# LRU half of the output projection: two pairs of tiles by seven quarter products over heads 0 to 3, and six conv tiles parked in DRAM

## Chip, cores, metric

The kernel runs on one core of a Trainium2 chip. The metric is the device time of one execution in microseconds (us), lower is better. Times before and after are medians of several runs; the profile is one further execution.

## The reference

One layer of a decoder trunk with 1024 channels and 1024 tokens (batch 1), in float32:

```python
mod = c_act @ mod_w[l] + mod_b[l]; shift, scale, gate = split(mod, 3)
h = rmsnorm(x, norm_g[l]) * (1.0 + scale) + shift
cv, cg, cs, lx, ls = split(h @ w_in[l], 5)              # five blocks of 1024 columns
v = cv * sigmoid(cg)
conv = (silu(layernorm(causal_depthwise_conv(v, 31 taps))) @ pw2 + pw2_b) * silu(cs)
xr = causal_depthwise_conv(lx, 4 taps)
r, i = sigmoid(xr_head @ wr_head + br), sigmoid(xr_head @ wi_head + bi)   # 8 heads of 128
h_t = a_t * h_{t-1} + sqrt(1 - a_t**2) * (i_t * xr_t)   # a_t from r_t, over the tokens
y = h * silu(ls)
x = x + (1 + gate) * (concat(conv, y) @ w_out)          # w_out: 2048 x 1024
out = rmsnorm(x, final_g)
```

The change concerns `y @ w_out[1024:]`, the half of the output projection that the LRU (recurrent) heads feed.

## The kernel before

**Layout.** Channels lie on the 128 partitions, tokens along the free dimension, so an activation of 1024 channels is eight tiles of 128 x 1024. A float32 product is three TensorE terms: each operand is split into a rounded high part (type fp32r) and the remainder (low part), and high x high, high x low and low x high are accumulated in PSUM. One output tile (128 channels x 1024 tokens) takes 8 contraction tiles x 3 terms x 2 halves of 512 tokens, 48 matmuls.

**Order.** All work is given to a planner (`class Plan`) as operations with an engine, a cost, a priority (about the slot number in which they are wanted) and the tiles that they read and write. It simulates the engines and writes out a fixed, in-order instruction stream for each: TensorE (PE), ScalarE (ACT), VectorE (DVE), GpSimd (POOL, which issues the accumulating DMAs) and SyncE (SP, which issues all other DMAs). Nothing is reordered at run time. An engine that waits holds up all that is behind it in its own stream. Tiles come from pools: 47 buffers of 128 x 1024 (`big`), two each for a raw weight tile (`raw`) and its high and low parts (`whi`, `wlo`), three PSUM tiles of 128 x 1024 and two of 128 x 512. A pool's buffer is handed on when its last reader is done.

**Stages.** After a start stage come 40 input tiles (`slots`, one slot each, 48 matmuls), between which eight gate groups stand. Meanwhile DVE, ACT and the accumulating DMAs (`es<-cq`, `oo<-co`) make the depthwise convolution of the conv tiles c0 to c7. Slots 40 to 47 are the eight `lru` tiles: TensorE multiplies the tile's weights with the eight heads (`yh`, `yl` are the high and low parts of y, contraction index k = head), DVE adds the gated result to x (`acc<-ps,gate,acc`, line 379 by way of a helper `STT`), and SP parks it in DRAM (`accd`). In the same stretch the layer norm of the conv tiles runs: `conv_sum` adds c0 to c7 into `csum` in the order `SUMS`, some by accumulating DMAs (`ADD`) and the last `CSD` ones by DVE (`TT`); `csum` is split into `csh` and `csl`, whose product with ones gives `mean`; then each tile has the mean subtracted, is squared into `lnss`, and scaled by `lnbc`. The next stage, `pw2`, is made in pairs of tiles by `pair_products`, with seven quarter products in place of eight, and so is the `out` stage that follows it.

**Weights of the LRU tiles.** `weights` loads a tile (`raw`) on SP 2.5 slots ahead; ACT rounds it to `whi`. From slot 41 on (`LATE`) the low part is made by `remainder`, which is ACT writing -whi to `wlo` and POOL issuing a DMA that adds the float32 weights from DRAM to it:

```python
ACT(prio, lo, lambda: hi().bitcast(F32), AF.Copy, n, scale=-1.0, r=rk, w=wk)
ADD(prio, lo, src, n, r=[*wk, *sk], w=wk, flight=LAND)
```

A tile's matmuls are issued by `mm_k`, one operation for each k. The functions named and their lines follow.

Of the kernel before, what the change touches and what calls it, by code (L numbers as in the profile page):

```python
# [9 lines left out]
F32 = mybir.dt.float32  # L10
F32R = mybir.dt.float32r
# [44 lines left out]
HOLDS = ()  # L56
LASTS = ((0, 3), (0, 1), (0, 1), (0, 3))
BCM = (512, 768)
QDMA = (('y',0,'T2'),('y',1,'T2'))
# [15 lines left out]
WOUT = ("DVE", "DVE", "DVE", "DVE")  # L75
AP = {0: (), 512: (1, 3, 5), 768: (1, 3, 5, 7)}
NP = {0: (6, 0, 1), 512: (6, 0, 7), 768: (6, 0)}
SUMS = (2, 3, 0, 1, 7, 4, 5, 6)
CSD = 4
EVN = 4  # L80
CQR = 2
YHEADS, YSLOT = 2, 36
QRES = 0
SINGLE = (0,)
AHEAD = 4
# [230 lines left out]
def hymba_layer(ctx: ExitStack, tc: tile.TileContext, xT, vecs, mod_w, w_first, w_in,  # L316
# [97 lines left out]
    def big_buf(name, dt=F32, parts=1):  # L414
        return S.buf("big", name, dt, parts)
# [38 lines left out]
    slots = list(FIRST + NEXT)  # L454
    for x in ORDER.split():
        slots.append(("gate" if x[0] == "g" else "in", int(x[1:])))
    slots += [("lru", m) for m in range(KT)]
    wslots = [s for s in slots if s[0] != "gate"] + [("out", m) for m in (4, 5, 6, 7)]
    number = {s: n for n, s in enumerate(wslots)}
    B0, C0, D0 = 40, 48, 56  # L460

# [10 lines left out]
    def k3(b):  # L472
        return lambda: b().rearrange("p (k c) -> p k c", k=KT)

    def remainder(prio, lo, hi, src, n, rk, wk, sk=()):
        ACT(prio, lo, lambda: hi().bitcast(F32), AF.Copy, n, scale=-1.0, r=rk, w=wk)
        ADD(prio, lo, src, n, r=[*wk, *sk], w=wk, flight=LAND)

    def w_slice(s, k, nk, p_load, p_prep, first_load=(), eng="POOL", late=()):
# [22 lines left out]
        w_bufs(s, where)  # L502
        w_slice(s, 0, KT, n - 2.5, n - 1.4, after, eng, late)

    def mm_k(prio, ps, s, xh, xl, k, cols, off=0, nk=KT, after=()):
        wh, wl = whi[s], wlo[s]

        def emit():
            for lhs, rhs, last in ((wh, xh, 0), (wh, xl, 0), (wl, xh, 1)):
                for a, b in cols:  # L510
                    pe.matmul(ps()[:, a - off:b - off], k3(lhs)()[:, k, :], rhs[k]()[:, a:b],  # L511
                              start=(k == 0 and lhs is wh and rhs is xh
                                     and (a - off) % H == 0),
                              stop=(k == nk - 1 and bool(last)), skip_group_check=True)
        n = sum(b - a for a, b in cols)
        rd = [(wh, k), (wl, k)]
# [645 lines left out]
    waiting = []  # L1162
    yh, yl = [None] * KT, [None] * KT

    def gw_load(i, n):
# [12 lines left out]
    def evac_in(m, ps, n, b=None, rb=()):  # L1178
        pr = n + 0.5
        kind, i = (m // KT) * KT, m % KT  # L1180
        if kind == CG:
            sig[i] = big_buf(f"sig{i}")
            ACT(pr, sig[i], ps, AF.Sigmoid, r=[ps], w=[sig[i]])
        elif kind == CV:
            sg = sig.pop(i)
            v[i] = big_buf(f"v{i}")
            TT(pr, "DVE", apart(v[i], 0, T), by_two(ps, 0, T), by_two(sg, 0, T), ALU.mult,
               r=[ps, sg], w=[v[i]])
        elif kind == CS:
            t = big_buf(f"scs{i}")  # L1190
            ACT(pr, t, ps, AF.Silu, bias=b, r=[ps, *rb], w=[t])
            scs_d[i] = dram.tile([P, T], F32, tag=f"scs{i}", name=f"scsd{i}")
            DMA(pr, lambda: scs_d[i], t, FULL_BYTES, r=[t], w=[("scsd", i)])
        elif kind == LS:
            sls[i] = big_buf(f"sls{i}")
            return ACT(pr, sls[i], ps, AF.Silu, bias=b, r=[ps, *rb], w=[sls[i]])
        else:
            xs, xh, xl = (big_buf(f"{a}{i}", d) for a, d in
                          (("xs", F32), ("xsh", F32R), ("xsl", F32R)))

            def w(s):
                o = SCW + i * STAPS + STAPS - 1 - s
                return V[:, o:o + 1]
            ACT(pr, xs, ps, AF.Identity, scale=w(0), bias=vec("sc_b", i), r=[ps], w=[xs])
            for s in range(1, STAPS):
                STT(pr, part(xs, s, T), part(ps, 0, T - s), w(s), part(xs, s, T), ALU.mult,
                    ALU.add, T - s, r=[ps, xs], w=[xs])
            split(pr + 0.2, xh, xl, xs)
            lru[i] = (xs, xh, xl)

    def gates(i, n):
        xs, xh, xl = lru[i]
        hi, lo = gw.pop(i)
        r, g, a = big_buf(f"r{i}"), big_buf(f"g{i}"), big_buf(f"a{i}")
        for j, (dst, b) in enumerate(((r, "br"), (g, "bi"))):
            ps = mm_tile(f"gate{i}_{j}")

            def emit(j=j, ps=ps):
                for lhs, rhs, st in ((hi, xh, 0), (hi, xl, 1), (lo, xh, 2)):
# [12 lines left out]
        TT(pr, "DVE", xs, xs, r, ALU.mult, r=[xs, r], w=[xs])  # L1232
        S.op("DVE", 2.2, lambda: dve.tensor_tensor_scan(
            out=r(), data0=a(), data1=xs(), initial=0.0, op0=ALU.mult, op1=ALU.add),
            pr, [a, xs], [r])
        t = sls.pop(i)
        TT(pr, "DVE", t, t, r, ALU.mult, r=[t, r], w=[t])
        yh[i], yl[i] = big_buf(f"yh{i}", F32R), big_buf(f"yl{i}", F32R)
        o = split(B0 - 2 + 0.2 * i, yh[i], yl[i], t, reserve=SPARE)
        if i < YHEADS:  # L1240
            waiting.append(o)

    def gate_mod(j, n, after):
        mod_load(2 * KT + j, n - 1, after)
# [304 lines left out]
```

## Time and profile before

| | |
|---|---|
| median of 3 runs | 731.97 us (731.78 to 733.33) |
| profiled execution | 731.52 us, span 729.70 us |
| granted TensorE clock | 0.997 |
| busy PE / DVE / ACT / POOL | 721.4 / 611.5 / 460.0 / 145.9 us |

The profile is one execution, recorded by the hardware. Its span runs from the first to the last recorded instruction; the execution's own time is 1.82 us longer. PEld is TensorE's weight load, which overlaps its matmuls. "x<-y" is an operation that writes x from y, by the names in the program with buffer numbers left out; `L379` is a line of the kernel, and where a helper issues all operations of a kind, all of them have the helper's line.

### The profile page before, as it was taken

To read this page: it belongs to the slowest core of one execution; us is meant where nothing else is said; L and a number is where in the kernel's file an instruction comes from. 1 tells how busy PE (TensorE), PEld (TensorE's weight loads), DVE (VectorE), ACT (ScalarE), POOL (GpSimd) and SP (SyncE) were. 2 spreads that over 40 slices of the span, in tenths; PEclk is the share of its full clock that TensorE was granted. 3 is DMA by queue.
4 is the path that set the end of the run, shared out by engine and by line. 5 is a ranking of instruction groups with operands and counts; after the bars stand their busy time and mean duration, and the time that the engine had idled before them with its cause. 6 is when DMAs were issued, how large, how long until landed. Compare 5 with 4: busy or idle time off the path is not lost.

```text
span 729.7 us, 8957 instructions
## 1 busy us (share of the span) xinstructions
PE 721.4 (99%) x3292; PEld 600.3 (82%) x3292; DVE 611.5 (84%) x835; ACT 460.0 (63%) x580; POOL 145.9 (20%) x144
## 2 busy tenths in 40 slices
PE   9999999999999999999999999999999999999996
PEld 8888888888888888888888888888888888888885
DVE  7999999799789997588599999677986566999647
ACT  7650677456698958956859778545953345755322
POOL 0043012353443232232122111000000001010003
PEclk9999999999999999999999999999999999999998
DMA  9943023457899999899576744676566756784006
GB/s 335 407 170 122 0 102 65 98 114 162 193 226 211 258 234 217 174 230 212 109 165 131 156 101 124 177 203 178 161 175 176 216 121 137 217 214 181 16 15 217
DMA packets 40940, 122.61 MB, mean 168 GB/s; under 512 B 4544, under 2 KB 13248, under 8 KB 40896
## 3 DMA queue, kind: packets, MB, share of 16 engines
q0 software_dynamic: 15984, 45.27, 34.2%
q1 hardware_dynamic: 23904, 75.84, 30.9%
q10 hardware_dynamic: 1008, 0.92, 0.4%
q8 instruction: 26, 0.43, 0.2%
q14 instruction: 18, 0.15, 0.1%
HBM read 72.55 MB, written 12.58 MB: 117 GB/s over the span
## 4 chain that ended last, share of the span: by engine, by line
PE 95%; DMA 2%; ACT 1%; DVE 1%; POOL 0%; issue 0%; DVEq 0%; POOLq 0%
PE ps L511 62%; PE xpw L680 6%; PE xout L680 6%; PE first L807 5%; PE ypw L680 3%; PE gate L1221 3%; PE y L655 2%; PE zout L680 1%; PE zpw L680 1%; DMA wlo<-in_w_out_dram 1%; PE yout L680 1%; DMA es<-cq 1%; PE late L807 1%; DVE o L379 1%; PE token_stats L764 1%; ACT cq L368 0%
## 5 line engine op out<-in xcount | busy, mean ns | idle before, releaser
L511 PE MATMUL ps<-uh,whi 128*128 128x512 f32 x576 | 177.5, 389 | 0.1
L511 PE MATMUL ps<-ul,whi 128*128 128x512 f32 x576 | 177.4, 389 | 0.0
L511 PE MATMUL ps<-uh,wlo 128*128 128x512 f32 x576 | 177.3, 389 | 0.0
L511 PEld LDWEIGHTS ps<-uh,whi 128*128 128x128 f32 x576 | 108.0, 188 | 22.8 <-ACT scs L368 0.5
L511 PEld LDWEIGHTS ps<-ul,whi 128*128 128x128 f32 x576 | 108.1, 188 | 22.5
L511 PEld LDWEIGHTS ps<-uh,wlo 128*128 128x128 f32 x576 | 108.1, 188 | 22.5
L360 ACT CAST whi<-raw 128x1024 fp32r<-128x1024 f32 x44 | 45.8, 1047 | 62.9 <-PE ps L511 34.6
L392 POOL DMA_DIRECT2D es<-cq x45 | 42.4, 957 | 117.5 <-ACT cq L368 93.5
L387 POOL TENSOR_TENSOR wlo<-raw,whi 128x1024 fp32r<-128x1024 f32 x16 | 40.8, 2561 | 123.4 <-ACT whi L360 90.7
L368 ACT ACT_TABLE_LOAD x44 | 56.5, 1283 | 2.5 <-issue 1.0
L379 DVE SCALAR_TENSOR_TENSOR cacc<-v,V,cacc 128x511 f32<-128x511 f32 (+14 forms) x75 | 55.4, 739 | 0.3
L379 DVE SCALAR_TENSOR_TENSOR caccs<-v,V,caccs 128x511 f32<-128x511 f32 (+6 forms) x70 | 52.0, 743 | 1.1
L379 DVE SCALAR_TENSOR_TENSOR caccs<-c,wsum,caccs 128x511 f32<-128x511 f32 (+6 forms) x70 | 51.9, 741 | 0.6
L392 POOL DMA_DIRECT2D oo<-co x39 | 36.3, 947 | 72.1 <-ACT co L368 30.3
L511 PE MATMUL ps<-yh,wlo 128*128 128x512 f32 x128 | 39.5, 390 | 0.2 <-DMA wlo<-in_w_out_dram 0.2
L511 PE MATMUL ps<-yh,whi 128*128 128x512 f32 x128 | 39.6, 391 | 0.0
L511 PE MATMUL ps<-yl,whi 128*128 128x512 f32 x128 | 39.5, 389 | 0.0
L368 ACT ACTIVATE cq<-v,V 128x511 f32<-128x511 f32 (+14 forms) x45 | 31.8, 707 | 0.0
L379 DVE SCALAR_TENSOR_TENSOR xs<-ps,V,xs 128x1023 f32<-128x1023 f32 (+2 forms) x24 | 30.6, 1274 | 0.0
L387 DVE TENSOR_TENSOR wlo<-raw,whi 128x1024 fp32r<-128x1024 f32 x21 | 25.6, 1218 | 5.7 <-ACT whi L360 5.6
L368 ACT ACTIVATE cq<-c,wsum 128x512 f32<-128x512 f32 x42 | 29.7, 711 | 0.0
L379 DVE SCALAR_TENSOR_TENSOR modw<-modw,sc 128x1024 f32<-128x1024 f32 x23 | 29.5, 1285 | 0.2 <-DMA modw<-in_mod_w_dram 0.2
(335 smaller groups left out, 1449.0 us busy)
## 6 DMA issues: line engine op xcount, KB each, us to landing
raw<-in_w_in_dram SPq DMA_DIRECT2D x36, 512.0 KB, 4.6
modw<-in_mod_w_dram SPq DMA_DIRECT2D x24, 512.0 KB, 8.5
scsd<-scs SPq DMA_DIRECT2D x8, 512.0 KB, 5.8
raw<-in_w_out_dram SPq DMA_DIRECT2D x8, 512.0 KB, 4.0
accd<-acc SPq DMA_DIRECT2D x8, 512.0 KB, 4.1
rawpw<-in_pw_dram SPq DMA_DIRECT2D x8, 512.0 KB, 4.5
scsr<-scsd SPq DMA_DIRECT2D x8, 512.0 KB, 4.8
rawout<-in_w_out_dram SPq DMA_DIRECT2D x8, 512.0 KB, 3.6
```

The source lines that it names most:

```text
L360: act.copy(out(), in_())
L368: act.activation(out=out(), in_=in_(), func=func, **kw)
L379: dve.scalar_tensor_tensor(out=out(), in0=in0(), scalar=scalar, in1=in1(), op0=op0, op1=op1, accum_out=accum)
L387: lambda: e.tensor_tensor(out=out(), in0=a(), in1=b(), op=op), prio, r, w,
L392: return S.op("POOL", ISSUE, lambda: pool.dma_start(out(), a(), accum_op=ALU.add), prio, r, w, lag=RATE * n / T, after=after, flight=flight)
L511: pe.matmul(ps()[:, a - off:b - off], k3(lhs)()[:, k, :], rhs[k]()[:, a:b], start=(k == 0 and lhs is wh and rhs is xh and (a - off) % H == 0),
L655: pe.matmul(to(), half(*lhs)()[:, j * P:j * P + P], half(*rhs)()[:, c0:c1], start=a == "S1" and j == 0 and t == 0, stop=j == KT // 2 - 1 a ...
L680: pe.matmul(half(ps, 0)(), half(*lhs)()[:, j * P:j * P + P], half(*rhs)(), start=start and j == 0 and t == 0, stop=j == KT // 2 - 1 and t ...
L764: pe.matmul(psb()[:, :P], ones, ones, start=True, stop=True)
L807: pe.matmul(ps()[:, a - off:b - off], fw_part(lhs, k, i * P, i * P + P)(), rhs()[:, a:b], start=k == 0 and lhs is wh and rhs is xh, stop=k ...
L1221: pe.matmul(ps()[:, c0:c1], lhs()[:, j, :], rhs()[:, c0:c1], start=st == 0, stop=st == 2)
```

## The change

The LRU tiles 0 to 3 are no longer four plain tiles but two pairs. Within a pair, the contraction over heads 4 to 7 stays plain. The contraction over heads 0 to 3 is seen as a 2 x 2 block product: weights A11, A12 (first tile of the pair, heads 0 and 2, heads 1 and 3) and A21, A22 (second tile), activations B11, B12 (heads 0 and 2, tokens 0 to 511 and 512 to 1023) and B21, B22 (heads 1 and 3). It is made from seven products of 6 matmuls instead of eight: A11 B11, A12 B21, S1 T1, S2 T2, S3 T3, S4 B22, A22 T4, where S are sums of weight blocks and T sums of activation blocks. `lru_sums` makes T in place from y (four half subtractions on DVE for each pair of heads j) and splits it again into high and low parts; for j = 1 the low parts go by `remainder`, that is by ACT and an accumulating DMA. `lru_pair` loads both tiles, makes S in the raw tiles (four additions or subtractions of 128 x 256 on DVE), splits S (`ls`), and issues the products in the order `LORDER`: p and q, r are the plain parts (24, 12 and 12 matmuls; p for both halves of tile 0 into PSUM `lp`, q for half 1 of tile 1 into `ly`, r for its half 0 into `lx`), and 1, z, y, 2, 3, s, 4 are the seven products. A product that several outputs share is read from PSUM while it stands in its accumulator, each time by one `STT` of 128 x 512 on DVE: eight for a pair. On the host the rows of the LRU half of `w_out` are put in the order `LK`.

To find room for the sums, six conv tiles (`SPILL`) are stored to DRAM by SP when they are complete (`cd`) and loaded again (`cr`) after slot 39 has begun. The order `SUMS` is another, and two conv tiles instead of four are added to `csum` by DVE, five instead of three by accumulating DMAs. The splits of heads 2 and 3, as those of 0 and 1 before, are held until slot 36 (`YHEADS`). `lru` tiles 4 to 7 and all other stages are issued as before.

The diff, with the unchanged middle of `mm_k` and a few small lines left out:

```diff
@@ -75,11 +75,17 @@
 WOUT = ("DVE", "DVE", "DVE", "DVE")
 AP = {0: (), 512: (1, 3, 5), 768: (1, 3, 5, 7)}
 NP = {0: (6, 0, 1), 512: (6, 0, 7), 768: (6, 0)}
-SUMS = (2, 3, 0, 1, 7, 4, 5, 6)
-CSD = 4
+SUMS = (2, 0, 4, 3, 1, 6, 7, 5)
+CSD = 2
+SPILL, SPP0, SPP1, SPN = (0, 2, 4, 3, 1, 6), 30, 40.5, 39
 EVN = 4
 CQR = 2
-YHEADS, YSLOT = 2, 36
+YHEADS, YSLOT = 4, 36
+JS, LRU_P = (0, 1), 2
+NJ = len(JS)
+LK = tuple(2 * j + z for z in (0, 1) for j in JS) + tuple(k for k in range(KT) if k // 2 not in JS)
+LORDER = "p1zy2q3s4r"
+LTP, LTD, LWD = 0.2, (2,1), ()
 QRES = 0
 SINGLE = (0,)
 AHEAD = 4
@@ -454,8 +460,8 @@
     slots = list(FIRST + NEXT)
     for x in ORDER.split():
         slots.append(("gate" if x[0] == "g" else "in", int(x[1:])))
-    slots += [("lru", m) for m in range(KT)]
-    wslots = [s for s in slots if s[0] != "gate"] + [("out", m) for m in (4, 5, 6, 7)]
+    wslots = [s for s in slots if s[0] != "gate"] + [("lru", m) for m in range(KT)]
+    slots += [("pair", p) for p in range(LRU_P)] + [("lru", m) for m in range(2 * LRU_P, KT)]
     number = {s: n for n, s in enumerate(wslots)}
     B0, C0, D0 = 40, 48, 56
 
@@ -472,8 +478,8 @@
     def k3(b):
         return lambda: b().rearrange("p (k c) -> p k c", k=KT)
 
-    def remainder(prio, lo, hi, src, n, rk, wk, sk=()):
-        ACT(prio, lo, lambda: hi().bitcast(F32), AF.Copy, n, scale=-1.0, r=rk, w=wk)
+    def remainder(prio, lo, hi, src, n, rk, wk, sk=(), reserve=0):
+        ACT(prio, lo, lambda: hi().bitcast(F32), AF.Copy, n, scale=-1.0, r=rk, w=wk, reserve=reserve)
         ADD(prio, lo, src, n, r=[*wk, *sk], w=wk, flight=LAND)
 
     def w_slice(s, k, nk, p_load, p_prep, first_load=(), eng="POOL", late=()):
@@ -502,18 +508,19 @@
         w_bufs(s, where)
         w_slice(s, 0, KT, n - 2.5, n - 1.4, after, eng, late)
 
-    def mm_k(prio, ps, s, xh, xl, k, cols, off=0, nk=KT, after=()):
+    def mm_k(prio, ps, s, xh, xl, k, cols, off=0, first=0, final=KT - 1, after=()):
         wh, wl = whi[s], wlo[s]
+        at = LK.index(k) if s[0] == "lru" else k
 
...
@@ -1150,16 +1157,22 @@
 
     def conv_sum():
         a = c[SUMS[0]]
-        ACT(1000 + 5 * SUMS[1], csum, a, "copy", r=[a, c[SUMS[1]]], w=[csum])
+        ACT(1000 + 5 * SUMS[1], csum, a, "copy", r=[a, c[SUMS[2]]], w=[csum])
         for i in SUMS[1:]:
             if i in SUMS[-CSD:]:
                 TT(1000 + 5 * i, "DVE", csum, csum, c[i], ALU.add, r=[csum, c[i]], w=[csum])
             else:
                 ADD(1000 + 5 * i, csum, c[i], r=[csum, c[i]], w=[csum])
+        for z, i in enumerate(SPILL):
+            cd = dram.tile([P, T], F32, tag=f"c{i}", name=f"cd{i}")
+            o = DMA(SPP0 + 0.1 * z, lambda cd=cd: cd, c[i], FULL_BYTES, r=[c[i]], w=[("cd", i)])
+            t = big_buf(f"cr{i}", parts=2)
+            DMA(SPP1 + 0.1 * z, t, lambda cd=cd: cd, FULL_BYTES, r=[("cd", i)], w=[t], after=[started[SPN]])
+            c[i] = t
 
 
...
@@ -1235,10 +1248,117 @@
             pr, [a, xs], [r])
         t = sls.pop(i)
         TT(pr, "DVE", t, t, r, ALU.mult, r=[t, r], w=[t])
-        yh[i], yl[i] = big_buf(f"yh{i}", F32R), big_buf(f"yl{i}", F32R)
+        yh[i], yl[i] = big_buf(f"yh{i}", F32R, 2), big_buf(f"yl{i}", F32R, 2)
         o = split(B0 - 2 + 0.2 * i, yh[i], yl[i], t, reserve=SPARE)
         if i < YHEADS:
             waiting.append(o)
+        if LRU_P and i // 2 in JS:
+            ys[i] = t
+            if i % 2:
+                lru_sums(i // 2)
+
+    def lru_sums(j):
+        pr, x0, x1 = B0 - 2 + 0.4 * j + LTP, ys[2 * j], ys[2 * j + 1]
+
+        def sub(to, a, b):
+            TT(pr, "DVE", half(*to), half(*a), half(*b), ALU.subtract, H, r=[a, b], w=[to])
+        sub((x0, 0), (x0, 1), (x0, 0))
+        sub((x0, 1), (x1, 1), (x0, 1))
+        sub((x1, 1), (x1, 1), (x0, 0))
+        sub((x1, 0), (x1, 0), (x1, 1))
+        sets = []
+        for z, x in enumerate((x0, x1)):
+            hi, lo = (big_buf(f"y{h}s{j}{z}", F32R, 2) for h in "hl")
+            if j in LTD:
+                ACT(pr, hi, x, "copy", r=[x], w=[hi], reserve=SPARE + 1)
+                remainder(pr, lo, hi, x, T, [hi], [lo], [x], SPARE)
+            else:
+                split(pr, hi, lo, x, reserve=SPARE)
+            sets.append((hi, lo))
+        a, b = 2 * j, 2 * j + 1
+        (c, d), (e, f) = sets
+        for q, hi, lo, z in (("B11", yh[a], yl[a], 0), ("B21", yh[b], yl[b], 0), ("B22", yh[b], yl[b], 1),
+                             ("T1", c, d, 0), ("T3", c, d, 1), ("T4", e, f, 0), ("T2", e, f, 1)):
+            lsets.setdefault(q, []).append(((hi, z), (lo, z)))
+
+    def lru_pair(p, n, use):
+        rest = LK[2 * NJ:]
+        s0, s1 = ("lru", 2 * p), ("lru", 2 * p + 1)
+        q = n - 1.4
+        for s in (s0, s1):
+            w_bufs(s)
+            DMA(n - 2.5, k3(raw[s]), lambda s=s: wsrc(s)[:, :, :], FULL_BYTES, w=[raw[s]])
+        r0, r1 = raw[s0], raw[s1]
+        for s, k in ((s0, 0), (s1, NJ)):
+            hi, lo, r = whi[s], wlo[s], raw[s]
+            cut = lambda b, k=k: (lambda: k3(b)()[:, k:, :])
+            keys = lambda b, k=k: [(b, i) for i in range(k, KT)]
+            ACT(q, cut(hi), cut(r), "copy", (KT - k) * P, r=keys(r), w=keys(hi))
+            remainder(q, cut(lo), cut(hi), lambda s=s, k=k: wsrc(s)[:, k:, :], (KT - k) * P, keys(hi), keys(lo))
+        w_ = NJ * P
+
+        def block(b, i):
+            return part(b, i * w_, i * w_ + w_)
+
+        def kk(b, i):
+            return [(b, k) for k in range(i * NJ, i * NJ + NJ)]
+
+        def comb(i, to, a, b, op):
+            TT(q + 0.01 * i, "DVE", block(*to), block(*a), block(*b), op, w_, r=kk(*a) + kk(*b), w=kk(*to))
+        comb(0, (r0, 0), (r0, 0), (r1, 0), ALU.subtract)
+        comb(1, (r0, 3), (r1, 0), (r1, 1), ALU.add)
+        comb(2, (r0, 2), (r1, 1), (r0, 0), ALU.subtract)
+        comb(3, (r0, 1), (r0, 1), (r0, 2), ALU.subtract)
+        sh, sl = (big_buf(f"ls{h}{p}", F32R) for h in "hl")
+        ACT(q + 0.1, sh, r0, "copy", r=[r0], w=[sh])
+        if p in LWD:
+            remainder(q + 0.1, sl, sh, r0, T, [sh], [sl], [r0])
+        else:
+            SUB(q + 0.1, "DVE", sl, r0, sh, T, [r0, sh], [sl])
+        wq = {"S3": (sh, sl, 0, 0), "S4": (sh, sl, 1, 0), "S2": (sh, sl, 2, 0), "S1": (sh, sl, 3, 0),
+              "A11": (whi[s0], wlo[s0], 0, None), "A12": (whi[s0], wlo[s0], 1, None),
+              "A22": (whi[s1], wlo[s1], 1, None)}
+        p0, x, y = mm_tile(f"lp{p}"), mm_tile(f"lx{p}"), acc_tile(f"ly{p}")
+        g, ops = 0.0, {}
+
+        def quarter(c, a, b, ps, h, begin):
+            wh, wl, i, key = wq[a]
+            rk = [(wh, key), (wl, key)] if key is not None else kk(wh, i) + kk(wl, i)
+            for j, (bh, bl) in enumerate(lsets[b]):
+                def emit(j=j, bh=bh, bl=bl):
+                    o = (i * NJ + j) * P
+                    for lhs, rhs, t in ((wh, bh, 0), (wh, bl, 1), (wl, bh, 2)):
+                        pe.matmul(half(ps, h)(), lhs()[:, o:o + P], half(*rhs)(),
+                                  start=begin and j == 0 and t == 0, stop=j == NJ - 1 and t == 2,
+                                  skip_group_check=True)
+                o = S.op("PE", 3 * (H + 32) / 2400, emit, n + g, [*rk, bh, bl],
+                         [(ps, h if ps.parts > 1 else 0)], columns=3 * H)
+                ops.setdefault(c, o)
+
+        for c in LORDER:
+            g += 0.12
+            if c == "p":
+                for k in rest:
+                    o = mm_k(n + g, p0, s0, yh, yl, k, FULL, first=rest[0])
+                    ops.setdefault(c, o)
+            elif c == "q":
+                for k in rest:
+                    mm_k(n + g, y, s1, yh, yl, k, FULL[1:], off=H, first=-1)
+                use(n, 1, 1, half(y, 0), (y, 0))
+            elif c == "r":
+                for k in rest:
+                    mm_k(n + g, x, s1, yh, yl, k, FULL[:1], first=-1)
+                use(n, 1, 0, half(x, 0), (x, 0))
+            else:
+                a, b, ps, h, begin, i, z = {
+                    "1": ("A11", "B11", x, 0, True, 0, 0), "z": ("A12", "B21", p0, 0, False, 0, 0),
+                    "2": ("S2", "T2", x, 0, False, 0, 1), "3": ("S3", "T3", x, 0, False, 1, 1),
+                    "y": ("S1", "T1", y, 0, True, 0, 1), "s": ("S4", "B22", p0, 1, False, 0, 1),
+                    "4": ("A22", "T4", x, 0, False, None, 0)}[c]
+                quarter(c, a, b, ps, h, begin)
+                if i is not None:
+                    use(n, i, z, half(ps, h), (ps, h if ps.parts > 1 else 0))
+        return ops["p"], ops["2"]
 
     def gate_mod(j, n, after):
         mod_load(2 * KT + j, n - 1, after)
@@ -1312,6 +1432,22 @@
             gates(s[1], n + 0.9)
             continue
         n += 1
+        if s[0] == "pair":
+            ts = [big_buf(f"acc{m}", parts=2) for m in (2 * s[1], 2 * s[1] + 1)]
+            for m, t in zip((2 * s[1], 2 * s[1] + 1), ts):
+                for z in (0, 1)[:1 + (m == 0)]:
+                    x_load(n - 1, t, m, z, [started[n - 2]])
+
+            def use(n, i, h, ps, key, s=s, ts=ts):
+                m, to, tk = 2 * s[1] + i, half(ts[i], h), (ts[i], h)
+                STT(n + 0.5, to, ps, gate1[:, m:m + 1], to, ALU.mult, ALU.add, H,
+                    r=[tk, key, ("gate1", m)], w=[tk])
+            started[n], started[n + 1] = lru_pair(s[1], n, use)
+            for m, t in zip((2 * s[1], 2 * s[1] + 1), ts):
+                acc_d[m] = dram.tile([P, T], F32, tag=f"acc{m}", name=f"accd{m}")
+                DMA(n + 0.5, lambda m=m: acc_d[m], t, FULL_BYTES, r=[t], w=[("accd", m)])
+            n += 1
+            continue
         if s not in NEXT:
             weights(s, late=[pending_evac[n]] if n in pending_evac else ())
         if GM <= n < GM + 8:
@@ -1535,7 +1671,7 @@
-        "w_out": np.concatenate([by_parity(tiles(w_out[:D])), tiles(w_out[D:])]),
+        "w_out": np.concatenate([by_parity(tiles(w_out[:D])), tiles(w_out[D:])[:, :, LK]]),
```

More of the change, by code (lines that the diff above doesn't have):

```diff
@@ L58 @@
 BCM = (512, 768)
-QDMA = (('y',0,'T2'),('y',1,'T2'))
+QDMA = (('y', 0, 'T2'), ('y', 1, 'T2'))
 DMAS = (("out", 1),)
@@ L510, in emit @@
                 for a, b in cols:
-                    pe.matmul(ps()[:, a - off:b - off], k3(lhs)()[:, k, :], rhs[k]()[:, a:b],
-                              start=(k == 0 and lhs is wh and rhs is xh
+                    pe.matmul(ps()[:, a - off:b - off], k3(lhs)()[:, at, :], rhs[k]()[:, a:b],
+                              start=(k == first and lhs is wh and rhs is xh
                                      and (a - off) % H == 0),
-                              stop=(k == nk - 1 and bool(last)), skip_group_check=True)
+                              stop=(k == final and bool(last)), skip_group_check=True)
         n = sum(b - a for a, b in cols)
-        rd = [(wh, k), (wl, k)]
+        rd = [(wh, at), (wl, at)]
         wr = []
@@ L1158, in conv_sum @@
                 ADD(1000 + 5 * i, csum, c[i], r=[csum, c[i]], w=[csum])
+        for z, i in enumerate(SPILL):
[4 more added lines that the diff above has]
+            c[i] = t
     sig, sls, lru, y, scs_d, gw = {}, {}, {}, {}, {}, {}
-    waiting = []
+    waiting, ys, lsets = [], {}, {}
     yh, yl = [None] * KT, [None] * KT
@@ L1194, in evac_in @@
         elif kind == LS:
-            sls[i] = big_buf(f"sls{i}")
+            sls[i] = big_buf(f"sls{i}", parts=2)
             return ACT(pr, sls[i], ps, AF.Silu, bias=b, r=[ps, *rb], w=[sls[i]])
```

## The prediction

> **What bounds the kernel now.** I read the page's busy shares first, then its clock row, its chain, and PE's own waits.
>
> ```profile
> PE 721.4 (99%) x3292; PEld 600.3 (82%) x3292; DVE 611.5 (84%) x835; ACT 460.0 (63%) x580; POOL 145.9 (20%) x144
> ...
> PEclk9999999999999999999999999999999999999998
> ...
> PE 95%; DMA 2%; ACT 1%; DVE 1%; POOL 0%; issue 0%; DVEq 0%; POOLq 0%
> ```
>
> TensorE is busy for 721.4 of 729.7 us, its granted clock is full in all slices but the last, and 95% of the chain that ended last is its own work. Its waits are three, 2.2 us in all:
>
> ```profile
> PE token_stats L764 <- DVE ones L437: 1.1, 1, 1.1
> PE finbc L729 <- DVE rs65.7_0_5712 L738: 0.9, 1, 0.9
> PE ps L511 <- DMA wlo<-in_w_out_dram: 0.2, 1, 0.2
> ```
>
> So the time is the number of matmuls times their pitch, and a matmul taken out is worth its pitch as long as nothing else comes late. The third wait lies at the head of the stretch that is changed. The chain there reads:
>
> ```profile
> 470.34 1.05 ACT whi L360
> ...
> 473.95 8.76 DMA wlo<-in_w_out_dram
> 482.75 0.73 PE ps L511 x2
> ...
> 504.81 1.73 PE lnbc L723 x16
> ...
> 509.82 53.09 PE ps L511 x234
> 562.91 2.72 PE xpw L680 x12
> ```
>
> Columns: start, length, engine and line. 234 matmuls in 53.09 us are 0.2269 us each, the pitch that I use. The low part of the second LRU weight tile is released when slot 39 ends (about 470.3), is cast, negated and sent to an accumulating DMA at 473.95, and lands 8.76 us later, 0.2 us too late. That is the one place in this stretch where TensorE has no reserve.
>
> **The change part by part.** *Fewer matmuls.* Two plain tiles are 96 matmuls. A pair is 24 (p) + 12 (q) + 12 (r) + 7 products of 6, that is 90. Two pairs save 12: 12 x 0.2269 = 2.72 us, all on the path. In the order of the changed kernel TensorE's instructions differ in this stretch alone, apart from one group of 6 that moves past a gate group. Gain 2.72, and the wait of 0.2 goes with the tile that it belonged to (the new waits there are costed next).
>
> *Two accumulating DMAs at the head of pair 0.* They stand where one stood. Before, ACT and the POOL queue did this:
>
> ```profile
> 470.34 1.05 ACT L360 CAST whi<-raw 128x1024 fp32r<-128x1024 f32 x1 [4.17 <-PE ps L511]
> 471.29 1.02 ACT L368 ACTIVATE scs<-ps 128x1024 f32<-128x1024 f32 x1
> 472.21 1.05 ACT L368 ACTIVATE wlo<-whi 128x1024 fp32r<-128x1024 f32 x1
> ...
> 478.46 1.05 ACT L360 CAST csh<-csum 128x1024 fp32r<-128x1024 f32 x1 [4.11 <-DVE csum L387]
> ```
>
> ```profile
> DMA to landing us min/median/max: 5.6/7.8/8.8
> ```
>
> The last row is the landing of the seven `wlo` tiles of the LRU stretch. After the change ACT has, from about 470.6, the copy of the last summed head (`yhs`), `whi` of tile 1, the negation for that head's low part (`yls`, head pair 1) and the negation for `wlo` of tile 1. At about a microsecond each, as above, with the hand-over that the old `wlo` took to its issue (472.21 to 473.95), the two DMAs issue near 473.55 and 474.45. TensorE runs p, 1, z, y, the two mean groups (0.9 us with four matmuls) and then 2. Its second head needs `yls` after 24 + 18 + 3 matmuls and more: 470.4 + 45 x 0.2269 + 0.9 = 481.5, and two matmuls later for the term itself, near 481.7. q needs `wlo` in its third term: 470.4 + 50 x 0.2269 + 0.9 = 482.65. With the median landing (7.8) both are there, 481.35 and 482.25: no wait. With 8.76 `yls` lands at 482.3, 0.6 late, and `wlo` at 483.2, which the shifted q just meets: 0.6 in all. The far end is the longest landing of an accumulating DMA in the crowded middle of the kernel, 11.0 (the row stands below): `yls` at 484.55, 2.85 late, and nothing more for q. So 0 to 2.85. I take 1.2, a little over the chain's own 8.76, because this time two go out a microsecond apart and the reloads of parked tiles are on the same engines.
>
> [...]
>
> *VectorE.* Rows for the new pieces:
>
> ```profile
> L379 DVE SCALAR_TENSOR_TENSOR acc<-ps,gate,acc 128x1024 f32<-128x1024 f32 x8 | 10.2, 1280 | 5.5 <-PE ps L511 5.5
> ...
> L387 DVE TENSOR_TENSOR yl<-sls,yh 128x1024 fp32r<-128x1024 f32 x5 | 5.8, 1220 | 0.6 <-ACT yh L360 0.6
> ...
> L387 DVE TENSOR_TENSOR csum<-csum,c 128x1024 f32<-128x1024 f32 x4 | 4.9, 1223 | 0.1
> ...
> L387 DVE TENSOR_TENSOR vu<-c,vt 128x512 f32<-128x512 f32 x4 | 2.7, 686 | 0.0
> ```
>
> ```profile
> L379 DVE SCALAR_TENSOR_TENSOR fin<-xout,gate,fin 128x512 f32<-128x512 f32 x16 | 11.9, 747 | 7.9 <-PE xout L680 7.9
> ...
> L387 DVE TENSOR_TENSOR glo<-graw,ghi 128x256 fp32r<-128x256 f32 x8 | 3.3, 420 | 2.2 <-ACT ghi L360 2.2
> ```
>
> ```profile
> 460.00:480.00 20.00, 20.00 (x90) 16.57 (x89) 11.43 (x11) 11.23 (x13) 0.89 (x1) 1.00 0.63 177
> ...
> 481.00:563.00 82.00, 81.79 (x377) 67.82 (x376) 67.85 (x75) 51.88 (x58) 7.00 (x8) 1.00 0.65 171
> ```
>
> The columns after the stretch and its length are busy PE, PEld, DVE, ACT and POOL (with instructions), clock, DMA share and GB/s. In the pairs 16 half evacuations at 0.747 replace 4 of 1.280 (+6.8), 8 block combinations at 0.42 (+3.4) and 2 low parts at 1.22 (+2.4) are new: 12.6 us, some 3 of them (pair 0's) before 481. DVE has 82 - 67.85 = 14.15 us idle there, so about 9.7 fit and hide under TensorE. Ahead of that come 8 half subtractions at 0.686 (+5.5), two `yls` by subtraction (+2.4) and pair 0's share (+2.9), against two `csum` additions fewer (-2.4): +8.4 against 8.57 idle in 460:480 and some before. This is full, and `csum` comes last in it: I get its end near 478.3, its high part near 479.4 where TensorE asks at 479.9, and the low part near 480.8 where it asks at 481.0. Between 0 and 1.2 (one instruction more in that queue); I take 0.1, since the order puts it in time. If this cover goes, all matmuls behind the mean wait too, and so does the layer norm, whose `lnbc` (504.81) would find the sum of squares just ready.
>
> ACT's additions are four `yhs` copies and two negations ahead of the pairs (6 x 1.05 = 6.3, against 20 - 11.23 = 8.8 us idle in 460:480) and two `ls` copies in them (2.1, against 30 idle): hidden, but for the two DMAs above that wait behind them. The outputs parked by `accd` issue twice per pair instead of once per tile, same bytes; the reload of conv tile 6 stands behind the first of them on SP, issues about 490 and is needed near 498: hidden.
>
> *Parks.* Six conv tiles go out and come back, 12 transfers of 512 KB on SP's queue, and two `csum` additions more are accumulating DMAs. The reloads fall into DMA shares of 0.63, the parks of c2 and c4 and the two additions into the stretch from 200 to 340:
>
> ```profile
> 220.00:240.00 20.00, 19.89 (x88) 16.16 (x87) 19.96 (x28) 16.95 (x20) 5.50 (x7) 1.00 1.03 227
> 240.00:260.00 20.00, 20.00 (x90) 16.55 (x89) 20.00 (x25) 15.92 (x23) 7.18 (x9) 1.00 1.03 250
> ...
> 280.00:300.00 20.00, 20.00 (x90) 16.57 (x89) 11.30 (x12) 17.41 (x20) 5.07 (x6) 1.00 0.82 176
> ```
>
> ```profile
> DMA to landing us min/median/max: 4.6/7.2/11.0
> ```
>
> ```profile
> 219.41 6.65 DMA es<-cq
> ...
> 227.41 0.92 ACT scs L368
> ...
> 228.38 1.66 PE ps L511 x6
> ```
>
> The middle row gives the landings of the 26 accumulating `es` DMAs of 200 to 340: they scatter by 6 us, and TensorE's waits show none of it. Against that, the chain goes through one of them at 219.41 and through ACT's evacuation to TensorE's restart at 228.38. At about 232 GB/s a transfer of 512 KB is 2.25 us, four are 9.0; 280:300 has 0.18 x 20 = 3.6 spare. So 0 to 5.4 for TensorE; a gain has no reason. I take 0.3, near the lower end, since landings up to 11.0 passed unseen.
>
> **Sum.** Against the profiled execution of 731.52 (span 729.70 and 1.82 around it): -2.72 - 0.2 + 1.2 + 0.1 + 0.3 = -1.3, that is 730.2. It stands 0.45 under the median of 731.97 (731.78 to 733.33), about their scatter, and I leave it so. What a measurement can tell from no change is about 0.2%, 1.46 us: faster is below 730.51, slower above 733.43.
>
> **The rivals.**
> - *No new wait.* Both landings at the median or below, parks unseen: 731.52 - 2.92 = 728.6. For it: the median of 7.8 suffices. Against: the chain's own instance, at this very place, took 8.76.
> - *The gain is eaten at pair 0.* Landings of 11.0 there, +2.85, and the sum chain on DVE +0.4: 728.6 + 3.25 = 731.85, no difference. For it: 5 reloads come in about this time, and DVE's queue is full in 460:480. Against: 0.63 DMA share.
> - *Slower: the parks back up the conv accumulations.* The park of c2 goes out near 225, into shares of 1.03; each `es` landing behind it is later, ACT waits for it in order with `scs` and `whi` queued behind that wait, and TensorE has no free buffer, as at 228.38. Full price 5.4: 728.6 + 1.2 + 5.4 = 735.2. It decides once more than 733.43 - 729.8 = 3.6 of the 5.4 reach TensorE. For it: the 0.11 us that TensorE already loses in 220:240. Against: the unseen scatter above. [...]
>
> That the change doesn't do what it says I leave out: the order has 90 matmuls in a pair.
>
> **How the numbers follow.** Forecast 0.45 (own range 729.3 to 731.2, from waits of 0.3 to 2.2), no wait 0.17, eaten 0.18, slower 0.20. Of the forecast's 0.45 three quarters (0.34) are below 730.51; with 0.17 that is faster 0.51. The rest, 0.11 and 0.18, is same 0.29; slower 0.20. The range goes from 728.8 (a third of the no-wait case lies below) to 733.6, which leaves out about two thirds of the slower case: some 0.06 and 0.13.
>
> **What the profile after would show.** Right: 12 matmuls fewer, pw2's first product near 561.6 (562.91 - 2.92 + 1.6), a wait of `lx` or `ly` for `yls` or `wlo` of 0.3 to 2.2 us near 481, none before 460. Wrong: a wait for `scs` or `whi` in 220 to 340, a mean group late behind `csum`, or a pitch other than 0.2269 in the quarter products.

## The result, and the profile after

The changed kernel takes 734.23 us (median of 22, 732.18 to 737.91), the kernel before 731.67 beside it (730.77 to 733.33): a ratio of 1.0035, 95% interval 1.0025 to 1.0044. It is 2.6 us slower where 1.8 faster was forecast, above the range that ends at 733.6. Its profiled execution took 732.40 (span 730.6), one of its shortest. One execution each of e2 (1168 us), e6 (1041) and the kernel before (1484) was slow as a whole: it counts in the medians below, and not in ranges, ratios and mean clocks.

TensorE's part of the page and its waits:

```profile
PE 719.7 (99%) x3280; PEld 598.3 (82%) x3280; DVE 625.2 (86%) x864; ACT 467.8 (64%) x589; POOL 150.3 (21%) x149
```

```profile
PE ly L518 <- DMA wlo<-in_w_out_dram: 2.0, 1, 2.0
PE token_stats L771 <- DVE ones L443: 1.1, 1, 1.1
PE finbc L736 <- DVE rs65.7_0_5781 L745: 0.9, 1, 0.9
PE xout L687 <- DMA wloout<-in_w_out_dram: 0.7, 1, 0.7
```

The 12 matmuls are gone (3292 to 3280). The wait of 0.2 has become one of 2.0 at the same place, and a wait of 0.7 in the out stage is new. The chain of the changed kernel goes through that landing, and pw2 starts 0.28 earlier (562.63 for 562.91), where 1.3 was forecast:

```profile
473.68 0.38 POOL yls L398
474.06 0.60 issue
474.66 0.01 POOLq L398
474.67 10.38 DMA wlo<-in_w_out_dram
485.05 0.04 issue
485.10 2.58 PE ly L518 x10
...
562.63 2.72 PE xpw L687 x12
```

The issue, 474.67, is where I had put it (474.45). The landing is 10.38 us later: over the 5.6 to 8.8 of the rows that I went by, though under the 11.0 that I gave as the far end. The two windows below, of the kernel before and then of the changed one, show what was different there (columns as in the prediction; the last two are the DMA share and GB/s). Behind each stand its DMA queues, with packets, MB and share of the 16 engines: q0 carries POOL's accumulating DMAs, q1 those of SP.

```profile
466.00:486.00 20.00, 19.79 (x87) 16.06 (x87) 9.22 (x10) 7.34 (x9) 1.77 (x2) 1.00 0.49 142
```

```profile
q1 hardware_dynamic: 627, 2.31, 35.8%
q0 software_dynamic: 144, 0.52, 13.2%
```

```profile
466.00:486.00 20.00, 18.00 (x80) 14.47 (x79) 19.56 (x23) 14.40 (x17) 3.49 (x4) 1.00 1.01 290
```

```profile
q1 hardware_dynamic: 1078, 3.97, 54.4%
q0 software_dynamic: 541, 1.82, 46.7%
```

The DMA engines went from half busy to full: 2.85 MB to 5.80 MB in 20 us. In the 10.38 us of the landing itself, 474.67 to 485.05, they moved 3.02 MB, of which the `wlo` that TensorE waits for is 0.39 (768 of 1024 columns).

The time of one execution goes, loosely, with its mean granted clock. Of 42 executions of this program (these, and those of e1 and e7), 18 had a clock of 0.996 or more and a median of 733.1; 13 had 0.994 or 0.995 and 734.2; 11 had 0.993 or less and 735.2. The mean is 0.9948 over the 30 of the result and e1, and 0.9964 over 31 of the kernel before. This mean holds two things. At the end of every trace here, from a moment between 722.2 us (e8) and 730.0 (e7) on, the clock is 0.50; by this end alone the mean is 0.995 (e8) to 0.998 (e2). A halving in the middle of the kernel, 3.4 us long in the three traces that have one, takes off another 0.0023. None of 110 executions of the kernel before lies under 0.995; 17 of these 42 do, so by an estimate from these numbers at least these had such a halving.

### The profile page after: what moved, and what is told of

Read it like the earlier page. It is cut to its first block, busy times and chain, and to the rows that moved or that the text cites. A ratio compares the mean times of both kernels' runs of the same rounds, so it can differ in the third digit from the quotient of the medians.

```text
span 730.6 us, 9023 instructions
## 1 busy us (share of the span) xinstructions
PE 719.7 (99%) x3280; PEld 598.3 (82%) x3280; DVE 625.2 (86%) x864; ACT 467.8 (64%) x589; POOL 150.3 (21%) x149
## 4 chain that ended last, share of the span: by engine, by line
PE 92%; DMA 3%; issue 2%; DVE 2%; ACT 0%; POOL 0%; DVEq 0%; POOLq 0%; ACTq 0%
PE ps L518 58%; PE xout L687 5%; PE first L814 5%; PE xpw L687 5%; PE gate L1234 3%; PE ypw L687 3%; PE y L662 2%; DMA wlo<-in_w_out_dram 1%; DMA wloout<-in_w_out_dram 1%; PE zpw L687 1%; PE lx L1331 1%; PE zout L687 1%; PE yout L687 1%; PE ly L518 1%; PE lx L518 1%
## 5 line engine op out<-in xcount | busy, mean ns | idle before, releaser
L366 ACT CAST whi<-raw 128x1024 fp32r<-128x1024 f32 (+1 forms) x44 | 45.3, 1035 | 42.7 <-issue 28.7
L398 POOL DMA_DIRECT2D es<-cq x45 | 41.7, 943 | 92.2 <-ACT cq L374 59.0
L374 ACT ACTIVATE uh<-x,shift 128x512 fp32r<-128x512 f32 x16 | 10.6, 715 | 26.2 <-PE ps L518 26.1
L374 ACT ACTIVATE co<-v,V 128x510 f32<-128x510 f32 (+12 forms) x39 | 26.8, 707 | 0.0
L374 ACT ACTIVATE finsq<-fin 128x512 f32<-128x512 f32 (+2 forms) x14 | 7.8, 569 | 26.6 <-DVE fin L385 13.4
```

The costliest lines, as they stand in the source:

```text
L366: act.copy(out(), in_())
L374: act.activation(out=out(), in_=in_(), func=func, **kw)
L398: return S.op("POOL", ISSUE, lambda: pool.dma_start(out(), a(), accum_op=ALU.add), prio, r, w, lag=RATE * n / T, after=after, flight=flight)
```

## The experiments

Each ratio is to the kernel before on the same chip.

**e1: the changed kernel again.** No edit.

> The changed kernel once more, for its scatter and a second trace. Theory A (the wait at the head of pair 0): the low part of the second tile of pair 0 lands 9 to 13 us after its issue, and TensorE waits 1.5 to 5 us there, more in the longer runs; nothing is lost before 460. Theory B (the parks back up the conv accumulations): TensorE waits for scs, whi or wlo between 200 and 340 in the longer runs. Both: about 734.2, from 732.2 to 737.9.

734.20 (733.0 to 736.91), ratio 1.0032 (1.0018 to 1.0046), mean clock 0.9936. The waits of its trace that are new against before, and the layer norm's second small group:

```profile
PE ly L518 <- DMA wlo<-in_w_out_dram: 1.4, 1, 1.4
...
PE ps L518 <- ACT scs L374: 0.3, 1, 0.3
PE lnbc L730 <- DVE lnss L393: 0.2, 1, 0.2
```

```profile
513.76 0.52 PE L1331 MATMUL lx<-yhs,wlo 128*128 128x512 f32 x1
514.08 3.48 PE L736 MATMUL lnbc<-ident,rs-1_0_4117 128*128 128x128 f32 x16
```

The wait at pair 0 is there again. The second group takes 3.48 us instead of the 1.95 of the changed kernel's first trace: the granted clock is 0.50 from 513.9 to 517.3, half of which is 1.7 us lost, and no wait shows it.

**e2: the low part of the second tile of each pair by GpSimd.** In `lru_pair`:

```diff
-            remainder(q, cut(lo), cut(hi), ...)
+            if k: SUB(q, "POOL", cut(lo), cut(r), cut(hi), ...)
+            else: remainder(q, cut(lo), cut(hi), ...)
```

> The low part of the second tile of each pair (768 columns) is made by a subtraction on GpSimd (about 1.9 to 2.6 us) instead of ACT's negation and an accumulating DMA; all else as in the changed kernel. Theory A: the 2.0 us of ly waiting for wlo go, and 1.8 us or more of the changed kernel's median with them: about 731.0 to 732.2, and the scatter of 5.7 us shrinks to under 2.5. Theory B: about 734, scatter as before.

733.17, ratio 1.0020 (1.0008 to 1.0031): about 1.0 less than e1 beside it, with intervals that overlap, not 1.8, and the scatter stays (731.7 to 736.0): a miss. The other accumulating DMA took the place of the removed wait:

```profile
PE lx L1334 <- DMA yls<-sls: 1.6, 1, 1.6
PE lx L1334 <- DVE acc L385: 1.2, 1, 1.2
```

This `yls`, issued at 474.25, lands 10.13 us later with no second accumulating DMA behind it, in a stretch (466:486) with a DMA share of 1.00.

**e3: the parks without the pairs.** `LRU_P` 2 to 0; eight plain LRU tiles.

> All eight LRU tiles plain, but the six conv tiles parked and reloaded and the new order of the csum additions kept. Theory A: no more than the accumulating DMA of the second LRU tile suffers, 731.7 to 732.7. Theory B: the price of the parks in full, 734 to 737 (the pairs' gain of 2.7 is missing), with waits between 200 and 340.

732.42, ratio 1.0006 (0.9998 to 1.0015). From the first gate group to the first LRU matmul its trace takes 354.3 us; the kernel before takes 354.0, the three traces of the changed one 353.8 to 354.5. The parks cost TensorE nothing there that these runs can tell; the slower rival is refuted. As the whole kernel without the pairs is about 1.8 faster than with them, it is the pairs, with the parks beside them, that lose. The `wlo` at this place lands in 6.9 us here, at a share of 0.76 in 466:486, and nothing waits for it.

**e4: the order of the sums alone.** `LRU_P` 0 and `SPILL` empty.

> All eight LRU tiles plain, no conv tile parked; only the new order of the csum additions, with five instead of three by accumulating DMAs, and the splits of heads 2 and 3 held. Both theories: 731.7, within 0.5 of before. If it is over 733, the additions are what backs up the accumulations, not the parks.

733.42, ratio 1.0023 (1.0015 to 1.0032), a miss for both theories. Its trace has waits for `wlo` (1.0), `whi` (0.5) and others in places where neither before nor e3 has any. With no parks the planner writes out another order of ACT, VectorE and GpSimd than in e3, so the 1.7 us over the kernel before are no price of the additions alone: e3 has the same additions, and parks besides, and is 1.0 faster. That points to the order, by a microsecond or more; and e2, e5, e10 and e11 are planned anew too: their streams differ from the changed kernel's in more than the edit.

**e5: the low parts of the second tiles and of the summed heads by GpSimd.** As e2, and in `lru_sums`:

```diff
-                remainder(pr, lo, hi, x, T, [hi], [lo], [x], SPARE)
+                SUB(pr, "POOL", lo, x, hi, T, [x, hi], [lo])
```

> The low parts of the second tile of each pair and of the summed heads of head pair 1 are all made by subtractions on GpSimd; no accumulating DMA is left at the head of pair 0. Theory A1 (only the wait at pair 0 costs): no wait of TensorE for wlo or yls, median 734.2 - 2.0 - 1.2 or more: 730.0 to 731.2, mean granted clock back to before's 0.9964. Theory A2 (the clock is lost at the layer norm's small matmuls, whatever happens at pair 0): the wait goes but the mean clock stays near 0.995, 731.5 to 732.5.

731.01 (729.86 to 731.93), ratio 0.9989 (0.9980 to 0.9997): 3.2 us under the changed kernel's 734.2, 2.0 under the repeat of the changed kernel on e5's own chip (e7, 732.99), and 0.7 under the kernel before. Mean clock 0.9965, as before, no execution under 0.995, and 2.1 us of scatter. This bears out A1: with the wait go its length and the clock's loss. Of the accumulating DMAs for pair 0 only the first tile's low part is left, issued at 464.3.

```profile
PE lx L1334 <- DVE acc L385: 1.1, 1, 1.1
```

No wait for `wlo` or `yls` is left; one of 1.1 for VectorE's queue is, at 510.7 (not near 500, as I wrote in expecting e9). From the first LRU matmul to pw2 it takes 90.3 us, against 92.2 before and 91.8, 93.0 and 94.4 in the three traces of the changed kernel.

**e6 and e8: the second small group of the layer norm 12 matmuls later**, with e5 and with the changed kernel. In `rstd`:

```diff
-        op = S.op("PE", 0.22 * nb, spread, prio, ...)
+        op = S.op("PE", 0.22 * nb, spread, 43.5 if prio == -1 else prio, ...)
```

> As e5, and the second group of small matmuls of the layer norm (lnbc from ident, 16 of 128x128) stands 12 matmuls (2.7 us) further behind the first group. A1: as e5 within 0.4. A2: mean granted clock 0.997 or over, and 0.5 to 1.2 us faster than e5.

> The changed kernel with only the second small group of the layer norm 12 matmuls later. A2: mean granted clock 0.9964 or over instead of 0.9948, 733.0 (1.2 less). A1: no change, 734.2, clock 0.995.

e6: 731.29, clock 0.9965, as e5, but its trace has every instruction in e5's order. In e5 the plan had already put 9 matmuls between the two groups, where the changed kernel has 6, and the edit moved none of them: e6 repeats e5 and tests nothing else. Its ratio of 0.9993 (0.9984 to 1.0002) leaves open whether this order is faster than the kernel before at all. e8, with 18 between them: 734.26, clock 0.9948, as the changed kernel; its waits for `wlo` are 1.6 at pair 0 and 0.4 at pair 1. So moving the group did not bring the clock back, as A2 would have it, and that rests on e8 alone. The halving of e1 still lies at just this group.

**e7: later loads of x.** `x_load` of pair 1 after the second product of pair 0.

> The changed kernel with every instruction in the same order; only the loads of x for tiles 2 and 3 (1 MB on the SP queue, issued at 477 and 479) wait until the second product of pair 0 has begun (about 481). If the landing of 10 us comes from what is on the DMA engines beside it, it falls to 8.0 to 9.0 and the wait for wlo to 0 to 1.0: 732.5 to 733.5. If it comes from the accumulating queue itself, it stays 10: 734.2.

The edit moved nothing: instructions and waits came out the same, and the loads still issue at 477.5. So it is a repeat of the changed kernel, 732.99 (730.88 to 735.97), ratio 1.0016 (1.0003 to 1.0028), and it says nothing of the loads. Its trace is of its longest execution:

```profile
PE ly L518 <- DMA wlo<-in_w_out_dram: 2.0, 1, 2.0
...
PE lx L1331 <- DMA yls<-sls: 0.9, 1, 0.9
```

```profile
482.00:487.00 5.00, 2.11 (x9) 1.13 (x7) 4.05 (x5) 3.27 (x5) 0.87 (x1) 1.00 1.04 341
487.00:488.00 1.00, 1.00 (x4) 0.80 (x5) 0.54 (x1) 0.93 (x2) 0.00 (x0) 0.82 1.07 250
488.00:489.00 1.00, 1.00 (x3) 0.76 (x3) 0.00 (x0) 0.63 (x1) 0.00 (x0) 0.50 1.05 229
489.00:490.00 1.00, 1.00 (x4) 0.75 (x3) 0.00 (x0) 0.00 (x0) 0.00 (x0) 0.50 0.56 119
490.00:491.00 1.00, 1.00 (x4) 0.81 (x3) 0.00 (x0) 0.00 (x0) 0.00 (x0) 0.50 0.15 41
491.00:492.00 1.00, 1.00 (x5) 0.83 (x5) 1.00 (x2) 0.00 (x0) 0.00 (x0) 0.98 0.07 29
```

TensorE is busy for 2.11 of 5 us, both waits lie there, and right behind them its clock is 0.50 for 3.4 us, from 487.63 to 491.04. Here the wait costs 2.9 and then about 1.7 more. In the 3.41 us that end at the halving, 484.22 to 487.63, TensorE was busy for 1.46. That alone does not explain it: in the first trace of the changed kernel it was busy for 1.42 of the 3.42 us from 482.20 to 485.62, and the clock stayed 1.00 there and to 490. Nor does the clock halve behind the other waits at pair 0 (2.0 in the changed kernel, 1.4 in e1, 1.6 and 1.2 in e2, 1.6 in e8, 2.3 in e11). What makes the difference is not shown, and no run tested it.

**e9, e12, e15: more of VectorE's work to GpSimd**, on top of e5. e9: pair 1's four combinations and `lsl`; e12: the same with the reloads one slot earlier; e15: `lsl` alone.

```diff
-            TT(q + 0.01 * i, "DVE", block(*to), ...)
+            TT(q + 0.01 * i, "POOL" if p else "DVE", block(*to), ...)
-            SUB(q + 0.1, "DVE", sl, r0, sh, ...)
+            SUB(q + 0.1, "POOL" if p else "DVE", sl, r0, sh, ...)
```

> As e5, and pair 1's four weight combinations and the low part of its sums on GpSimd too, which takes some 2.9 us from VectorE between 486 and 494. If VectorE's queue is what makes e5's lx wait 1.1 us for acc near 500, that wait goes and the time is 729.6 to 730.3. If that wait has another cause, 731.0 as e5, or more where GpSimd's slow subtractions are late.

> e9 with e11's earlier reloads. With no accumulating DMA left at pair 0 the place of the reloads should not matter: as e9 within 0.5, clock 0.9965.

> e5 with only the low part of pair 1's weight sums moved from VectorE to GpSimd (the four combinations stay on VectorE). If e5's lx waits 1.1 us for acc because VectorE is full between 486 and 500, the wait falls to 0.5 or less: 730.2 to 730.7. If e9's result says that other waits follow at once, 731.0 to 731.3.

731.30, 731.30 and 731.70; ratios 1.0005 (0.9989 to 1.0021) for the first two and 0.9998 (0.9988 to 1.0007). In e15 the wait for `acc` stays (1.1). In e9 it is gone, and one for the next low part has come:

```profile
PE ps L518 <- DMA wlo<-in_w_out_dram: 1.1, 1, 1.1
```

Nothing is won over e5. What is left of the 2.7 us there goes, at least in part, to waits that replace one another. And e9 and e12 have long executions again, up to 737.3 and 737.1 at clocks of 0.990 and 0.993, without e5's two DMAs at pair 0; neither kept trace is of one, so what halves the clock there is not known.

**e10: only the summed heads by GpSimd.** The second edit of e5 without the first.

> Only the low parts of the summed heads by GpSimd; the low part of the second weight tile still by the accumulating DMA. If each of the two DMAs costs by itself, the wait for wlo stays (1 to 2 us) and the time is 732.5 to 733.5, between the changed kernel and e5 as e2 was. If two in a row are what makes them late, the wait falls to 0.5 and the time to 731 to 732.

735.48, ratio 1.0057 (1.0044 to 1.0070), clock 0.9912: worse than the changed kernel, e2 and e5, a miss. GpSimd's queue shows it:

```profile
467.09 10.39 POOL L393 TENSOR_TENSOR yls<-sls,yhs 128x1024 fp32r<-128x1024 f32 x2 [2.85 <-ACT yhs L366]
477.42 0.89 POOL L398 DMA_DIRECT2D wlo<-in_w_out_dram  x1
```

The two subtractions take 7.58 and 2.73 us, where the page's `wlo<-raw,whi` row has a mean of 2.56, and the DMA of `wlo` is queued behind them: issued 2.75 later than in the changed kernel. TensorE then waits 1.0 (at 486) and 0.9 (at 512) for low parts and 1.2 (at 514) for `lnss`, and right behind the last two the clock is 0.50, from 516.9 to 520.3. The `wlo` itself landed in 8.69 us, without `yls` ahead of it.

**e11: the reloads one slot earlier.** `SPP1, SPN` 40.5, 39 to 39.5, 38.

> The changed kernel with the reloads of parked tiles released one slot earlier, so that none of them is issued between 468 and 485; both accumulating DMAs stay. If the 10 us landing comes from the reloads beside it, it falls to 8 or less and the time to 732 or less. If it comes from the other transfers there, or from the accumulating DMA itself, the wait of 1.4 to 2.0 us stays: 734.

736.82, ratio 1.0067 (1.0055 to 1.0079). `yls` now lands 12.14 us after its issue and TensorE waits 2.3 for it. No reload issues from 468 to 485, but the loads of weights and of x stand behind them on SP and moved into that place, and the two accumulating DMAs changed their order; the share in 480:490 is 1.05. Which transfer is to blame can't be told from this; that moving some of them does not empty the stretch can. This trace has no halving in the middle.

**e13 and e14: the kernel before with a later accumulating DMA.** One GpSimd instruction of 128 x 1024 between negation and DMA of the second LRU tile, and two; no other instruction moves. For e13, in short:

```diff
-            remainder(p_prep, cut(lo), cut(hi), ...)
+            ACT(p_prep, lo, hi, AF.Copy, scale=-2.0); POOL: lo = lo + hi; ADD(p_prep, lo, wsrc)
```

> The kernel before, every instruction in its order, with one GpSimd addition of 128x1024 (2.6 to 5 us) put between the negation of the second LRU tile's low part and its accumulating DMA, so that TensorE's wait of 0.2 at that place grows to 2.5 to 5. If a wait there costs its length only: 731.8 + 2.3 to 4.8, mean clock 0.9965. If the granted clock then halves for a while, as after a wait of 2.9 us in e7's trace: 1.0 to 1.7 us more than the wait in the runs where it does, mean clock 0.995 or less.

> As e13 with two such GpSimd instructions: the wait is 5 to 10 us. If only its length counts: 731.8 + 5 to 10, clock as before except for nothing. If the clock falls: it halves in every run for about 3.4 us after the wait, 1.7 us more than the wait, mean clock 0.994 or less and always so.

e13: 732.01, ratio 1.0000 (0.9991 to 1.0009), clock 0.9962. e14: 734.15, ratio 1.0028 (1.0017 to 1.0040), clock 0.9957. The chains, e13 first:

```profile
476.25 6.48 DMA wlo<-in_w_out_dram
482.78 0.73 PE ps L521 x2
```

```profile
479.44 5.43 DMA wlo<-in_w_out_dram
484.92 0.73 PE ps L524 x2
```

Issued 2.30 us later than before, the transfer lands at the same moment (476.25 + 6.48 = 482.73, before 473.95 + 8.76 = 482.71), and the wait stays 0.2 where I expected 2.5 to 5. Only the second instruction delays it, to a wait of 1.9 (5 to 10 expected). So of the 8.76, by an estimate from the two landings, at least 3.3 (8.76 - 5.43) was time in which it stood behind or shared with other transfers. The packets point the same way: in the kernel before, from the issue at 473.95 to 477.00, the accumulating queue moved nothing and SP's queue 0.89 MB at 88% of the engines; in e14 it moved nothing from 479.44 to 481.00 either, with the engines 4% busy, so not all of that time is the traffic's. And a single wait of 1.9 halves no clock in its trace; e14 lost little clock (0.9957 against 0.9966 beside it).

## Why the prediction was wrong, step by step

**Fewer matmuls**: right, 12 less, and pitch 0.2267 (2.72 for 12).

**Two accumulating DMAs at the head of pair 0**: this step failed. The place and the issue times were right, the size was not: I took 1.2, and the three traces of the changed kernel have 2.0, 1.4 and 2.9 there, e8 1.6. Nor was it the wait that I had summed: with a landing of 8.76 I had `yls` 0.6 late and `wlo` just met, but in the first trace `yls` is in time (8.17) and `wlo` late. I gave both DMAs the same landing, so that they came 0.9 apart; issued 1.00 apart, they landed 3.21 apart, in e1 2.94 and in e7 3.15. I took a landing from a trace in which the DMA engines were half empty, as if it belonged to the instruction. By the estimate from e14, at least 3.3 of its 8.76 belonged to the moment of its issue, not to the instruction (5.43 when issued 5.49 later). The change adds transfers at this very place, and for these I added next to nothing to the 8.76, by a share of 0.63 that was measured without them. With them it was 1.01 in 466:486, where it had been 0.49. That the fuller engines are what made the landing later is what these rows point to; no run kept the two DMAs and emptied the stretch. Nor is it shown how much of it comes from SP's transfers and how much from the neighbour on the same queue, though e2's `yls` was as late without one. In the changed kernel the two landings were 8.17 (`yls`) and 10.38 (`wlo`, 384 KB) in the first trace, 9.4 and 11.5 in e7.

**The wait's price**: I priced it by its length. Behind the waits of 2.9 us in e7 the clock halves and costs 1.7 more. The mean clock is 0.0016 under before's, 0.0016 x 731 = 1.2 us. That is the term that the sum had no line for. Executions under a clock of 0.995 are 17 of 42 for the changed kernel and 4 of 12 for e8, none of 32 for e5, e6 and e15, which have no such wait, and none of 110 for the kernel before. But of the three halvings caught in a trace only e7's lies at pair 0. Those of e1 and e10 lie at the layer norm's small matmuls, and e9 and e12 lose clock in 4 of 23 executions without the two DMAs. So how much of the lost clock is due to pair 0 stays open.

**VectorE**: hidden in the changed kernel, as said: 19.56 of 20 us are busy in 466:486, and TensorE waited 0.2 for it at most in this stretch. Once the DMAs are gone it is next (1.1 in e5).

**Parks**: 0.3 taken, none found before 470 (e3). What they cost comes with the reloads, inside the first failed step; by itself it was not measured.

**Out stage**: I had no term. `wloout` came 0.7 late in the first trace. In e1 and e7 this wait is absent, and e13, which has the out stage of the kernel before, has 0.4 of it: it comes and goes, and it stays unexplained.

The profiled execution nearly adds up: 731.52 - 2.92 + 2.0 (`wlo`) + 0.7 (`wloout`) gives 731.3 of 732.40. Of the other 1.1 the start has 0.2 (the first gate group begins at 116.81 for 116.59; over all traces here it begins between 116.2 and 117.5), the stretch of the pairs 0.6, the out stage 0.2 and the end behind the last matmul 0.2; 0.2 less went between the gates and the pairs. Part of the 0.6 is the wait itself: the matmuls around it start at 482.70 and 485.10, 2.4 apart instead of 0.23, so it cost 2.2. From there to the median of 734.2 lie the clock (about 1.2) and longer waits in other executions, of which e7's 2.9 is the one example. How these two share it is not settled. And without the two DMAs the gain still falls short: e5's stretch is 1.8 shorter than before's (90.3 for 92.2), not 2.9.

**The rivals**: that the gain would be eaten at pair 0 was the right place and the right cause, late landings, at 0.18, priced at 2.85 without the clock; the slower one, by parks in 200 to 340, was the right sign for a wrong reason.

## What to carry to other kernels

Before an added transfer is called hidden, add its bytes to the DMA share of the 20 us in which it lands; a landing time read in a half-empty stretch is a measure of that stretch (8.76 us at a share of 0.49 here, 10.38 at 1.01). In e7 TensorE lost 2.9 us in waits and then about 1.7 more at a clock of 0.50; a wait of 2.3 in e11 had no halving behind it. So a change that buys 2.7 us of matmuls loses more than that to two late arrivals like those of e7. Where an accumulating DMA is on the path, try the plain subtraction on an idle engine, for all such DMAs at that place together: for one alone the median was 1.0 lower (e2) or 1.3 higher (e10), for both 3.2 lower (2.0 against the repeat on the same chip). An edit that the planner turns into another order tests that order too: compare the instruction streams of the two traces before the result is put down to the edit, or a repeat (e6, e7) passes for a test.

## What the runs showed of the hardware

Two float32 subtractions of 128 x 1024 on GpSimd took 10.39 us in e10, 7.58 and 2.73, with VectorE busy for all of 460 to 480; the mean of 16 in the kernel before was 2.56. Why is not shown. POOL's accumulating DMAs took up the 16 engines about twice as long for their bytes as SP's DMAs, by the page of the changed kernel:

```profile
q0 software_dynamic: 16704, 47.63, 35.9%
q1 hardware_dynamic: 25632, 82.13, 32.3%
```

That is 0.75% of the span for a MB on the accumulating queue and 0.39% on SP's.

At pair 0 the clock was 0.50 for 3.4 us behind waits of 2.9 us (e7), and it stayed 1.00 behind waits of 1.2 to 2.3 (five other traces). At the layer norm's small matmuls (16 of 128x1) it was 0.50 from 513.9 to 517.3 in e1, with TensorE counted as busy for 3.23 of the 3.41 us before; in the first trace of the changed kernel and in e7 it stayed 1.00 from 500 to 520.
